# The last token block's norm of the convolution branch as a line of stages, and stores in part one given out some planned time behind their data

## The chip, the cores and the metric

The kernel runs on one core of one Trainium2 chip. The metric is the device time of one execution in microseconds, the median of several. The kernel before has a median of 2943.98 us in 3 runs (2941.24 to 2945.05). Engines are named as the profile names them: PE is TensorE, ACT ScalarE, DVE VectorE, POOL GpSimd, SP SyncE, which here only issues transfers (SPq in the timeline).

## The reference, cut to what matters

One layer of a streaming encoder works on 2048 prompt tokens and 64 sample tokens, 1024 channels wide:

```python
h = rms_norm(x, g1) * (1 + sc1) + sh1
z = h @ w_in                       # [GLU a | GLU b | q | k | v | gate conv | gate attn]
u = glu_a * sigmoid(glu_b)
conv = silu(layer_norm(depthwise31(u) + b_dw)) @ w_conv_out
attn = band_attend(rms_norm(q), rms_norm(k), v) @ w_attn_out
x = x + gt1 * ((sigmoid(g_conv) * conv + sigmoid(g_attn) * attn) @ w_o)
x = x + gt2 * swiglu(rms_norm(x, g2) * (1 + sc2) + sh2)
```

The change touches the layer norm with its swish on the convolution branch, the two sigmoid gates, and the attention result.

## The kernel before

**Part one** (0 to about 1163 us) makes `z` and both branches, **part two** multiplies by `w_conv_out`, `w_attn_out` and `w_o`, and the feed-forward network follows. Part one goes through four token blocks (0 to 576, 1088, 1600, 2112). In each of them PE makes, in this order, q, the convolution's first channel tile, k, the second, v, the third and fourth, and the gates (`g`). Activations and weights are split into a high and a low half in a rounded 32-bit type, so one product is a triple of matmuls: high by high, low by high, high by low. Everything that leaves for the chip's memory as an operand of a later product is therefore a pair of tiles, `part_h` and `part_l`. Pairs come from `parts()` (line 786), two buffers of each half for the whole of part one (NS = 2, line 781); plain temporaries come from `temp` (line 783), seven buffers.

PE's order in part one is the order of the code. The other work is written as generators that sit in lanes: normalising the next block, attention heads, the tail (layer norm) and the convolution. While the code issues PE's stages, a planner (`Stream`) adds up an estimated load for every engine, and each 500 ns of estimated PE time `tick` gives out what is due and then lets each lane take a step. `stream.when(engine)` is the planned time at which that engine has done its work so far; a generator that yields it isn't stepped before PE's planned time gets there. `stream.at(t, f)` runs `f`, here the issue of a store, when that time comes; `stream.flush()` runs all that is waiting, and the code calls it ahead of a new block's attention, in the last block ahead of the gates' last groups, and at the end of part one. So nothing but planned time decides where an instruction lands on its engine's in-order queue.

The rows of the profile all have line 105, since `Meter.run` records every call there; tiles tell them apart. Transfers keep their own lines:

- `conv_norm` (line 1296) takes a block's convolution output `y` through layer norm and swish, in four channel tiles of 128 x 512. Each is scaled by the deviation (POOL), goes through tanh into a tile `ln` (ACT), through two operations of DVE, and is split into a pair (ACT copies the high half, DVE or POOL subtracts for the low half). The pair is stored in `c_d` at line 1350. After each of these four steps the generator yields until the engine's planned time. It sits in the lane `tail`, for the last block added by the code at line 1706.
- `gates` (line 1354) takes the tanh of a gate column into a tile `gate` and stores it in `g_d` from ACT's own queue at once (line 1364).
- `finish_head` makes the attention result `o_p` of two heads, splits it and stores it in `o_d` (line 1460).
- In part two `merge` loads gate columns `tg` from `g_d` (line 1143) and operands `cin` from `c_d` and `o_d` (line 1151), makes 24 matmuls for each of eight channel tiles of the first 320 tokens (`ps<-cin`), and combines them on DVE (`t<-tg,ps`, then `ps<-ps,t`), four PSUM banks for all. The matmuls `pw` are the product with `w_o`. The pools of part two are opened when those of part one are closed (line 1716), and lie in the same memory: a first `t` must wait until the last store of part one has been read out.

In a head, PE makes scores (`sc`), DVE adds the bias (`pr<-sc,bias`), ACT takes the exponential, DVE the reciprocal, ACT scales, PE transposes (`ptp`), ACT and DVE split (`ph`, `pl`), and PE multiplies by the values (`po<-ph,vv`).

All other stores and all weight loads of part one go through SP's one in-order queue: a transfer whose data isn't there holds up everything issued behind it.

Of the kernel before, what the change touches and what calls it, by code (L numbers as in the profile page):

```python
# [8 lines left out]
F32 = mybir.dt.float32  # L9
# [23 lines left out]
QB = 512  # L33
# [18 lines left out]
FIRST_LAG = 14000.0  # L52
BIAS_LAG = 6000.0
OUT_LAG = 4000.0
CACHE_LAG = 16000.0
HEADS_NS = 2000.0
SIDE_G = 10
# [565 lines left out]
def streaming_layer(ctx: ExitStack, tc: tile.TileContext, I, O):  # L623
# [669 lines left out]
                )  # L1293
            yield

    def conv_norm(y, c0, n, t0):
        yv = y[:, :, c0 : c0 + n]
        yield lambda: not conv.gens
        s = wk.tile([P, 512], F32, tag="ln_s", bufs=1)

        def total():
            ps = ps_g.tile([P, 512], F32, tag="gp", name="pm")
            pe.matmul(ps[:, :n], ones, s[:, :n], start=True, stop=True)
            return ps

        gps.tensor_tensor(s[:, :n], yv[:, 0], yv[:, 1], ALU.add)
        for ct in (2, 3):
            gps.tensor_tensor(s[:, :n], s[:, :n], yv[:, ct], ALU.add)
        yield stream.when("pool") + PE_LAG
        pm = total()  # L1310
        yield stream.when("pe")
        for ct in range(4):
            dve.tensor_tensor(yv[:, ct], yv[:, ct], pm[:, :n], ALU.subtract)
        yield stream.when("dve")
        act.activation(s[:, :n], yv[:, 0], AF.Square)
        for ct in range(1, 4):
            tmp = temp("ln")
            act.activation(tmp[:, :n], yv[:, ct], AF.Square)
            yield stream.when("act")
            gps.tensor_tensor(s[:, :n], s[:, :n], tmp[:, :n], ALU.add)  # L1320
        yield stream.when("pool") + PE_LAG
        pm = total()
        yield stream.when("pe")
        act.activation(s[:, :n], pm[:, :n], AF.Sqrt, bias=eps_t)
        yield stream.when("act")
        for c in range(0, n, P):
            e = min(n, c + P)
            dve.reciprocal(s[:, c:e], s[:, c:e])
            yield
        yield stream.when("dve")  # L1330
        done = []
        for ct in range(4):
            gps.tensor_tensor(yv[:, ct], yv[:, ct], s[:, :n], ALU.mult)
            done.append(stream.when("pool"))
        for ct in range(4):
            yield done[ct]
            tmp = temp("ln")
            act.activation(tmp[:, :n], yv[:, ct], AF.Tanh, bias=lnh[:, 4 + ct : 5 + ct], scale=lnh[:, ct : ct + 1])
            yield stream.when("act")
            dve.tensor_scalar(yv[:, ct], yv[:, ct], lng[:, ct : ct + 1], lnb[:, ct : ct + 1], ALU.mult, ALU.add)  # L1340
            dve.scalar_tensor_tensor(tmp[:, :n], tmp[:, :n], 1.0, yv[:, ct], ALU.add, ALU.mult)
            yield stream.when("dve")
            hi, lo = parts()
            act.activation(hi[:, :n], tmp[:, :n], AF.Copy)
            yield stream.when("act")
            name = low(hi[:, :n], lo[:, :n], tmp[:, :n], n, TT_LESS)

            def store(ct=ct, hi=hi, lo=lo):
                for l, a in enumerate((hi, lo)):
                    nc.sync.dma_start(c_d[l, ct, :, t0 : t0 + n], a[:, :n].bitcast(F32))  # L1350

            stream.at(stream.when(name), store)

    def gates(b, free):

        o = PBLOCKS[b][0]
        w = PBLOCKS[b][1] - o

        def part(g, ws, c0, c1):
            ps = columns(*ws, kts(hh), kts(hl), c0, c1)  # L1360
            t = temp("gate")
            stream.after("act", "pe")
            act.activation(t[:, : c1 - c0], ps[:, : c1 - c0], AF.Tanh, scale=0.5)
            nc.scalar.dma_start(g_d[g // 8, g % 8, :, o + c0 : o + c1], t[:, : c1 - c0])

        def pair(g):
            ws = [W.get(("in", 2560 + g * P, h)) for h in range(2)]
            return [[[w[l][:, k, e * P : e * P + P] for w in ws for k in range(4)] for l in range(2)] for e in range(2)]

        n = 16 - SPLIT_G if b + 1 < len(PBLOCKS) else 16  # L1370
        for g in range(0, n, 2):
            for e, ws in enumerate(pair(g)):
                for c in halves(0, w):
                    part(g + e, ws, *c)
                if e:
                    W.done()
                    W.done()
                yield g + e
        rest = [ws for g in range(n, 16, 2) for ws in pair(g)]
        for c0, c1 in ((0, w // 2), (w // 2, w)):  # L1380
            for i, ws in enumerate(rest):
                part(n + i, ws, c0, c1)
                if c1 == w and i % 2:
                    W.done()
                    W.done()
            free["columns"] = c1
# [56 lines left out]
    def finish_head(h, po, n, q0, key):  # L1443
# [10 lines left out]
        if i:  # L1454
# [4 lines left out]
                for l, a in enumerate((hi, lo)):  # L1459
                    nc.sync.dma_start(o_d[l, h // 2, :, q0 : q0 + n], a[:, :n].bitcast(F32))  # L1460

            stream.at(stream.when("dve"), store)

    def spans(b):

# [182 lines left out]
    for b, stage in ORDER:  # L1648
# [44 lines left out]
        else:  # L1693
# [7 lines left out]
            if stage == 3:  # L1701
# [1 line left out]
                    tail.add(conv_norm(y, 0, SMP, 0))  # L1703
                    tail.add(conv_norm(y, SMP + HIST, QB, SMP))
                else:
                    tail.add(conv_norm(y, 0, QB, lo))
        for _ in range(MODS.get((b, stage), 0)):
            next(mods)
    next(mods)
# [672 lines left out]
```

## Time and profile before

| | us |
|---|---|
| median of 3 runs | 2943.98 (2941.24 to 2945.05) |
| the profiled execution | 2941.67 |
| its span, first to last instruction | 2939.5 |
| mean granted clock of PE in it | 0.997 |
| PE idle in the span | 50.2 |

The profiled execution lies 2.3 us under the median and 2.2 us above its own span. In a timeline a row has the start, the duration, the engine, line, operation, out<-in with the tiles' names, the shape, and in brackets how long the engine had been idle before it and what released it. A row of the stretch view has the stretch, its length, the busy time of PE, of PE's weight loads, of DVE, ACT and POOL (with counts), the granted clock of PE as a share of the full one, the share of the transfer engines and GB/s. In the view of waits a row has the waiting engine, tile and line, what it waited for, the total, the count and the longest. A row of the transfer view has the count, the size and the us from issue to landing.

### The profile page before, as it was taken

To read this page: it belongs to the slowest core of one execution; us is meant where nothing else is said; L and a number is where in the kernel's file an instruction comes from. 1 tells how busy PE (TensorE), PEld (TensorE's weight loads), DVE (VectorE), ACT (ScalarE), POOL (GpSimd) and SP (SyncE) were. 2 spreads that over 40 slices of the span, in tenths; PEclk is the share of its full clock that TensorE was granted. 3 is DMA by queue.
4 is the path that set the end of the run, shared out by engine and by line. 5 is a ranking of instruction groups with operands and counts; after the bars stand their busy time and mean duration, and the time that the engine had idled before them with its cause. 6 is when DMAs were issued, how large, how long until landed. Compare 5 with 4: busy or idle time off the path is not lost.

```text
span 2939.5 us, 44832 instructions
## 1 busy us (share of the span) xinstructions
PE 2889.3 (98%) x16193; PEld 2587.5 (88%) x16193; DVE 2053.9 (70%) x3648; ACT 1362.7 (46%) x2453; POOL 1164.9 (40%) x753
## 2 busy tenths in 40 slices
PE   7999999999999999999999999999999999999999
PEld 5899777888888887988999998999999999999998
DVE  5897788668967885577777756666666557566666
ACT  3346543751564266563444345444444345444442
POOL 1201210111011002553566452366567742465667
PEclk9999999999999999999999999999999999999999
DMA  9989899978996987984444875332333965333333
GB/s 322 315 305 314 287 281 329 285 232 306 285 297 197 320 270 224 291 295 157 144 144 146 292 261 200 97 122 94 115 115 104 346 220 179 97 103 106 115 107 127
DMA packets 467067, 628.04 MB, mean 214 GB/s; under 512 B 36196, under 2 KB 314584, under 8 KB 466845
## 3 DMA queue, kind: packets, MB, share of 16 engines
q1 hardware_dynamic: 452944, 606.11, 63.4%
q10 hardware_dynamic: 13901, 19.08, 1.9%
q8 instruction: 127, 2.08, 0.3%
q14 instruction: 95, 0.78, 0.1%
HBM read 476.53 MB, written 148.54 MB: 213 GB/s over the span
## 4 chain that ended last, share of the span: by engine, by line
PE 47%; DVE 2%; ACT 1%; DMA 1%; issue 1%; POOL 0%; SPq 0%; ACTq 0%; DVEq 0%; POOLq 0%
PE ps L105 29%; PE pd L105 13%; PE pw L105 5%; DVE wlo L105 1%; ACT whi L105 1%; DVE ps L105 0%; DMA cin<-o_d 0%; DMA x<-x_d 0%; DVE acc L105 0%; ACT xn L105 0%; DMA wst<-in_w_ffn_in 0%; DMA wfo<-in_w_ffn_out 0%; DMA tg<-g_d 0%; DVE sums L105 0%; PE pt L105 0%
## 5 line engine op out<-in xcount | busy, mean ns | idle before, releaser
L105 PE MATMUL ps<-t,whi 128*128 128x384 f32 (+1 forms) x2112 | 502.0, 322 | 2.8 <-ACT u L105 1.7
L105 POOL TENSOR_TENSOR wlo<-wst,whi 128x1024 fp32r<-128x1024 f32 (+1 forms) x159 | 362.7, 2293 | 246.1 <-ACT whi L105 214.4
L105 ACT ACTIVATE whi<-wst 128x1024 fp32r<-128x1024 f32 (+1 forms) x265 | 258.3, 979 | 316.1 <-PE ps L105 129.6
L105 PE MATMUL ps<-b,whi 128*128 128x384 f32 (+1 forms) x1584 | 380.7, 325 | 6.4 <-DVE v L105 2.1
L105 PEld LDWEIGHTS ps<-t,whi 128*128 128x128 f32 x2112 | 367.8, 188 | 10.1 <-ACT u L105 3.9
L105 DVE SCALAR_TENSOR_TENSOR y<-u,wd,y 128x512 f32<-128x512 f32 (+1 forms) x480 | 370.1, 774 | 8.0
L105 PE MATMUL ps<-hh,whi 128*128 128x512 f32 (+2 forms) x992 | 362.8, 366 | 0.1
L105 DVE TENSOR_TENSOR acc<-acc,pd 128x512 f32<-128x512 f32 x482 | 322.2, 685 | 48.1 <-PE pd L105 45.6
L105 PE MATMUL ps<-hh,wlo 128*128 128x512 f32 (+2 forms) x992 | 345.2, 348 | 0.0
L105 PE MATMUL ps<-hl,whi 128*128 128x512 f32 (+2 forms) x992 | 344.5, 347 | 0.0
L105 PE MATMUL ps<-t,wlo 128*128 128x384 f32 (+1 forms) x1056 | 338.5, 321 | 0.0
L105 PE MATMUL pd<-whi,hid 128*128 128x512 f32 x912 | 297.9, 391 | 0.6 <-DVE hid L105 0.3
L105 PEld LDWEIGHTS ps<-b,whi 128*128 128x128 f32 x1584 | 276.9, 188 | 14.6 <-DVE v L105 3.2
L105 ACT ACTIVATE pr<-pr,sm 128x640 f32<-128x640 f32 (+3 forms) x272 | 201.9, 749 | 137.1 <-DVE sm L105 134.8
L105 PE MATMUL ps<-b,wlo 128*128 128x384 f32 (+1 forms) x792 | 256.1, 323 | 0.0
L105 POOL TENSOR_TENSOR r<-t,mhalf 128x1 f32<-128x1 f32 (+2 forms) x68 | 82.3, 1219 | 403.7 <-DVE t L105 377.8
L105 PEld LDWEIGHTS ps<-hh,wlo 128*128 128x128 f32 x992 | 186.5, 188 | 22.6
L105 DVE TENSOR_TENSOR wlo<-wst,whi 128x1024 fp32r<-128x1024 f32 (+1 forms) x106 | 135.9, 1286 | 100.3 <-ACT whi L105 98.9
L105 PEld LDWEIGHTS pd<-whi,hid 128*128 128x128 f32 x912 | 171.2, 188 | 37.2 <-DVE acc L105 1.8
L105 PEld LDWEIGHTS ps<-hh,whi 128*128 128x128 f32 x992 | 187.0, 189 | 18.2 <-issue 3.3
L105 PEld LDWEIGHTS ps<-hl,whi 128*128 128x128 f32 x992 | 187.4, 189 | 14.3 <-issue 1.7
L105 PEld LDWEIGHTS ps<-t,wlo 128*128 128x128 f32 x1056 | 198.2, 188 | 0.8
(233 smaller groups left out, 6309.6 us busy)
## 6 DMA issues: line engine op xcount, KB each, us to landing
whi<-w_din_h SPq DMA_DIRECT2D x72, 512.0 KB, 6.4
wlo<-w_din_l SPq DMA_DIRECT2D x72, 512.0 KB, 7.3
wst<-sum_d SPq DMA_DIRECT2D x131, 256.0 KB, 3.1
wfo<-in_w_ffn_out SPq DMA_DIRECT2D x64, 512.0 KB, 4.1
wmod<-in_w_ada SPq DMA_DIRECT2D x46, 512.0 KB, 8.8
sum_d<-ws SPq DMA_DIRECT2D x88, 256.0 KB, 2.0
wst<-in_w_ffn_in SPq DMA_DIRECT2D x85, 256.0 KB, 3.2
wst<-in_w_in SPq DMA_DIRECT2D x40, 512.0 KB, 6.0
```

Source lines behind the costliest of these rows:

```text
L105: self.last = f(*args, **kw)
```

## The change

Three things are done, and no operation is added or taken away.

1. `conv_norm` of the **last block** runs as a line: seven steps with one yield each, in which channel tile i is scaled (POOL), tile i - 1 goes through tanh (ACT), tile i - 2 through DVE's two operations, and tile i - 3 is split and stored. The other blocks keep the old order.
2. The stores of `c_d`, and of `o_d`, are due 2000 ns of planned PE time later than before (`PART_LAG`).
3. The gates' stores on ACT's queue, formerly issued at once, are due 2000 ns after ACT's planned time.

```diff
@@ -52,6 +52,7 @@
 FIRST_LAG = 14000.0
 BIAS_LAG = 6000.0
 OUT_LAG = 4000.0
+PART_LAG = 2000.0
 CACHE_LAG = 16000.0
 HEADS_NS = 2000.0
 SIDE_G = 10
@@ -1293,7 +1294,7 @@
                 )
             yield
 
-    def conv_norm(y, c0, n, t0):
+    def conv_norm(y, c0, n, t0, line=False):
         yv = y[:, :, c0 : c0 + n]
         yield lambda: not conv.gens
         s = wk.tile([P, 512], F32, tag="ln_s", bufs=1)
@@ -1328,28 +1329,55 @@
             dve.reciprocal(s[:, c:e], s[:, c:e])
             yield
         yield stream.when("dve")
+        tmps = [None] * 4
+
+        def over(ct):
+            gps.tensor_tensor(yv[:, ct], yv[:, ct], s[:, :n], ALU.mult)
+
+        def swish(ct):
+            tmps[ct] = temp("ln")
+            act.activation(tmps[ct][:, :n], yv[:, ct], AF.Tanh, bias=lnh[:, 4 + ct : 5 + ct], scale=lnh[:, ct : ct + 1])
+
+        def times(ct):
+            tmp = tmps[ct]
+            dve.tensor_scalar(yv[:, ct], yv[:, ct], lng[:, ct : ct + 1], lnb[:, ct : ct + 1], ALU.mult, ALU.add)
+            dve.scalar_tensor_tensor(tmp[:, :n], tmp[:, :n], 1.0, yv[:, ct], ALU.add, ALU.mult)
+
+        def give(ct):
+            tmp = tmps[ct]
+            hi, lo = parts()
+            act.activation(hi[:, :n], tmp[:, :n], AF.Copy)
+            if not line:
+                yield stream.when("act")
+            name = low(hi[:, :n], lo[:, :n], tmp[:, :n], n, TT_LESS)
+
+            def store():
+                for l, a in enumerate((hi, lo)):
+                    nc.sync.dma_start(c_d[l, ct, :, t0 : t0 + n], a[:, :n].bitcast(F32))
+
+            stream.at(stream.when(name) + PART_LAG, store)
+
+        if line:
+            for i in range(7):
+                if 0 <= i - 3:
+                    yield from give(i - 3)
+                for step, ct in ((times, i - 2), (swish, i - 1), (over, i)):
+                    if 0 <= ct < 4:
+                        step(ct)
+                if i < 6:
+                    yield stream.when("act", "dve", "pool")
+            return
         done = []
         for ct in range(4):
-            gps.tensor_tensor(yv[:, ct], yv[:, ct], s[:, :n], ALU.mult)
+            over(ct)
             done.append(stream.when("pool"))
         for ct in range(4):
             yield done[ct]
-            tmp = temp("ln")
-            act.activation(tmp[:, :n], yv[:, ct], AF.Tanh, bias=lnh[:, 4 + ct : 5 + ct], scale=lnh[:, ct : ct + 1])
+            swish(ct)
             yield stream.when("act")
-            dve.tensor_scalar(yv[:, ct], yv[:, ct], lng[:, ct : ct + 1], lnb[:, ct : ct + 1], ALU.mult, ALU.add)
-            dve.scalar_tensor_tensor(tmp[:, :n], tmp[:, :n], 1.0, yv[:, ct], ALU.add, ALU.mult)
+            times(ct)
             yield stream.when("dve")
-            hi, lo = parts()
-            act.activation(hi[:, :n], tmp[:, :n], AF.Copy)
-            yield stream.when("act")
-            name = low(hi[:, :n], lo[:, :n], tmp[:, :n], n, TT_LESS)
-
-            def store(ct=ct, hi=hi, lo=lo):
-                for l, a in enumerate((hi, lo)):
-                    nc.sync.dma_start(c_d[l, ct, :, t0 : t0 + n], a[:, :n].bitcast(F32))
-
-            stream.at(stream.when(name), store)
+            yield from give(ct)
 
     def gates(b, free):
 
@@ -1361,7 +1389,10 @@
             t = temp("gate")
             stream.after("act", "pe")
             act.activation(t[:, : c1 - c0], ps[:, : c1 - c0], AF.Tanh, scale=0.5)
-            nc.scalar.dma_start(g_d[g // 8, g % 8, :, o + c0 : o + c1], t[:, : c1 - c0])
+            stream.at(
+                stream.when("act") + PART_LAG,
+                lambda: nc.scalar.dma_start(g_d[g // 8, g % 8, :, o + c0 : o + c1], t[:, : c1 - c0]),
+            )
 
         def pair(g):
             ws = [W.get(("in", 2560 + g * P, h)) for h in range(2)]
@@ -1459,7 +1490,7 @@
                 for l, a in enumerate((hi, lo)):
                     nc.sync.dma_start(o_d[l, h // 2, :, q0 : q0 + n], a[:, :n].bitcast(F32))
 
-            stream.at(stream.when("dve"), store)
+            stream.at(stream.when("dve") + PART_LAG, store)
 
     def spans(b):
 
@@ -1703,7 +1734,7 @@
                     tail.add(conv_norm(y, 0, SMP, 0))
                     tail.add(conv_norm(y, SMP + HIST, QB, SMP))
                 else:
-                    tail.add(conv_norm(y, 0, QB, lo))
+                    tail.add(conv_norm(y, 0, QB, lo, b == len(PBLOCKS) - 1))
         for _ in range(MODS.get((b, stage), 0)):
             next(mods)
     next(mods)
```

Where instructions land follows from the planner. A first place is **PE at the end of part one**, around the last scores. `sc` are scores of a head, `ps<-hh,whi` and the like triples of gate columns, `gates_c` a small transpose, `ptp` the transposes of a softmax. Before:

```order
L105 MATMUL sc<-kk,q_12193 128x320 x4
L105 MATMUL ps<-hh,whi 128x512
L105 MATMUL ps<-hl,whi 128x512
L105 MATMUL ps<-hh,wlo 128x512
L105 MATMUL ps<-hh,whi 128x512
L105 MATMUL ps<-hl,whi 128x512
L105 MATMUL ps<-hh,wlo 128x512
L105 MATMUL ps<-hh,whi 128x512
L105 MATMUL ps<-hl,whi 128x512
L105 MATMUL ps<-hh,wlo 128x512
L105 MATMUL ps<-hh,whi 128x512
L105 MATMUL ps<-hl,whi 128x512
```

The last of the twelve gate matmuls behind `sc`, then `gates_c` and twelve `ptp` follow these rows. Of the change:

```order
L106 MATMUL sc<-kk,q_12190 128x320 x4
L106 MATMUL ps<-hh,whi 128x512
L106 MATMUL ps<-hl,whi 128x512
L106 MATMUL ps<-hh,wlo 128x512
L106 MATMUL ps<-hh,whi 128x512
L106 MATMUL ps<-hl,whi 128x512
L106 MATMUL ps<-hh,wlo 128x512
L106 MATMUL sc<-kk,q_12190 128x320 x4
L106 MATMUL pt<-ident,gates_c 32x128
L106 MATMUL ptp<-ident,pr 128x128 x12
L106 MATMUL po<-ph,vv 128x512
```

Gate columns that stood behind the last `sc` stand ahead of it now; the two groups of scores have six gate matmuls between them, and `ptp` follows the second with only `gates_c` between.

The second place is **SP at the end of part one**: stores of the norm (`c_d`), of attention (`o_d`), loads of weights for part two (`wst`) and of gate columns (`tg`). Before:

```order
L1350 DMA c_d<-part_h 128x512
L1350 DMA c_d<-part_l 128x512
L1350 DMA c_d<-part_h 128x512
L384 DMA wst<-in_w_o 128x1024
L915 DMA gt_d<-row 32x128
L384 DMA wst<-in_w_o 128x1024
L1460 DMA o_d<-part_h 128x512
L1460 DMA o_d<-part_l 128x512
L1350 DMA c_d<-part_l 128x512
L1350 DMA c_d<-part_h 128x512
L1143 DMA tg<-g_d 128x320
L1350 DMA c_d<-part_l 128x512
```

Of the change:

```order
L1356 DMA c_d<-part_h 128x512
L1356 DMA c_d<-part_l 128x512
L1356 DMA c_d<-part_h 128x512
L1356 DMA c_d<-part_l 128x512
L1356 DMA c_d<-part_h 128x512
L1356 DMA c_d<-part_l 128x512
L385 DMA wst<-in_w_o 128x1024 x2
L916 DMA gt_d<-row 32x128
L1491 DMA o_d<-part_h 128x512
L1491 DMA o_d<-part_l 128x512
L1144 DMA tg<-g_d 128x320 x2
L385 DMA wup<-in_w_conv_out 128x4x128
```

The three c_d stores that stood behind the o_d pair or a weight load are all ahead now, and the o_d pair is part one's last; a `tg` load that stood between c_d stores stands behind it.

The third place is **SP at the seam from block 0 to block 1**: four pairs of the first blocks' norm (`c_d`), weights of the value projection (`whi`, `wlo` from w_dqkv_3) and of the next product (w_din), values (`vv`) and queries (`q_d`). Before:

```order
L1350 DMA c_d<-part_h 128x512
L1350 DMA c_d<-part_l 128x512
L1350 DMA c_d<-part_h 128x512
L1350 DMA c_d<-part_l 128x512
L479 DMA whi<-w_dqkv_3_h 128x1024
L1350 DMA c_d<-part_h 128x512
L1350 DMA c_d<-part_l 128x512
L479 DMA wlo<-w_dqkv_3_l 128x1024
L1350 DMA c_d<-part_h 128x512
L1350 DMA c_d<-part_l 128x512
L1436 DMA vv<-v_d 128x4x128
L1054 DMA q_d<-part_h 128x4x128
```

Of the change:

```order
L1356 DMA c_d<-part_h 128x512
L1356 DMA c_d<-part_l 128x512
L480 DMA whi<-w_dqkv_3_h 128x1024
L480 DMA wlo<-w_dqkv_3_l 128x1024
L1356 DMA c_d<-part_h 128x512
L1356 DMA c_d<-part_l 128x512
L1467 DMA vv<-v_d 128x4x128
L1356 DMA c_d<-part_h 128x512
L1356 DMA c_d<-part_l 128x512
L1356 DMA c_d<-part_h 128x512
L1356 DMA c_d<-part_l 128x512
L480 DMA whi<-w_din_h 128x1024
```

The second, third and fourth pair have moved behind both weight loads of the value projection, the third and fourth behind `vv` too.

## The prediction, made before the changed kernel ran

> **What bounds the kernel now.** I begin with the page's first part, to see whether any engine sets the end by itself.
>
> ```profile
> PE 2889.3 (98%) x16193; PEld 2587.5 (88%) x16193; DVE 2053.9 (70%) x3648; ACT 1362.7 (46%) x2453; POOL 1164.9 (40%) x753
> ```
>
> TensorE (PE) is busy for 2889.3 of a span of 2939.5 us, so all its waits together are 50.2 us, and the change alters no matmul. It can gain only from those waits and from a slow clock behind them. The view of PE's waits says whom it waited for.
>
> ```profile
> PE pt L105 <- DVE kn L105: 6.1, 2, 4.0
> PE ps L105 <- DVE t L105: 5.8, 5, 3.4
> ```
>
> The longest of each kind (4.0 and 3.4 us) lie at the two seams where the moved stores stand: the seam from token block 0 to block 1, and the seam from part one to part two. The timeline of PE, for both:
>
> ```profile
> 360.51 0.63 PE L105 MATMUL pt<-ident,kn 128*128 128x128 f32 x4 [3.96 <-DVE kn L105]
> ...
> 1152.59 0.74 PE L105 MATMUL sc<-kk,q 128*128 128x320 f32 x4
> 1153.17 0.39 PE L105 MATMUL ps<-hh,whi 128*128 128x512 f32 x1
> ...
> 1155.92 0.27 PE L105 MATMUL pt<-ident,gates_c 128*32 128x128 f32 x1
> ...
> 1157.02 1.20 PE L105 MATMUL ptp<-ident,pr 128*128 128x128 f32 x9 [0.50 <-ACT pr L105]
> ...
> 1164.57 0.56 PE L105 MATMUL ps<-cin,whi 128*128 128x320 f32 x2 [1.40 <-DVE o_p L105]
> ...
> 1171.57 0.31 PE L105 MATMUL ps<-cin,wlo 128*128 128x320 f32 x1
> ...
> 1175.29 0.90 PE L105 MATMUL ps<-cin,whi 128*128 128x320 f32 x2 [3.42 <-DVE t L105]
> ...
> 1201.09 0.40 PE L105 MATMUL pw<-whi,m 128*128 128x512 f32 x1
> ```
>
> The stretch view gives the granted clock behind such waits.
>
> ```profile
> 20.00:24.00 4.00, 3.87 (x28) 1.22 (x28) 2.04 (x4) 0.00 (x0) 0.00 (x0) 1.00 1.08 358
> ...
> 109.40:114.40 5.00, 5.00 (x26) 4.25 (x27) 5.00 (x7) 3.02 (x4) 0.00 (x0) 1.00 0.91 312
> ...
> 361.00:366.00 5.00, 5.00 (x19) 4.21 (x18) 2.71 (x6) 1.72 (x4) 0.00 (x0) 0.56 1.10 379
> 366.00:371.00 5.00, 5.00 (x24) 4.27 (x23) 4.54 (x10) 1.41 (x2) 0.00 (x0) 0.76 1.04 399
> ...
> 1175.30:1180.30 5.00, 5.00 (x19) 5.00 (x20) 2.88 (x7) 0.44 (x1) 0.00 (x0) 0.50 0.90 269
> ```
>
> The third number from the right is the clock. After the wait of 3.96 it was 0.56 and then 0.76, after that of 3.42 it was 0.50. So a long wait is paid twice: 5.0 x 0.44 + 5.0 x 0.24 = 3.4 us more at the first seam, 5.0 x 0.50 = 2.5 us more at the second. Two shorter or earlier waits cost nothing more:
>
> ```profile
> 20.13 1.08 PE L105 MATMUL pa<-wmod,cl 128*32 128x256 f32 x8 [3.44 <-DMA wmod<-in_w_ada]
> ...
> 109.40 0.63 PE L105 MATMUL pt<-ident,kn 128*128 128x128 f32 x4 [2.15 <-DVE kn L105]
> ```
>
> The clock stayed at 1.00 behind 2.15 and, at the start, behind 3.44. The point from which it falls thus lies above 2.15 and about 3.4, and is not sharp.
>
> **The second seam, before.** Part two's first tiles lie in the memory of part one's, so VectorE's `t` waits for part one's last store to land. SyncE's rows (SPq), VectorE's (DVE) and GpSimd's (POOL) in one timeline:
>
> ```profile
> 1154.52 0.32 SPq L1350 DMA_DIRECT2D c_d<-part_h  x1
> ...
> 1164.67 0.55 DVE L105 TENSOR_SCALAR y<-y,cols 128x512 f32<-128x512 f32 x1 [0.15 <-ACT ln L105]
> 1165.25 0.69 DVE L105 SCALAR_TENSOR_TENSOR ln<-ln,y 128x512 f32<-128x512 f32 x1
> ...
> 1166.57 0.32 SPq L1460 DMA_DIRECT2D o_d<-part_l  x1
> ...
> 1169.43 2.39 POOL L105 TENSOR_TENSOR wlo<-wst,whi 128x1024 fp32r<-128x1024 f32 x1 [5.71 <-ACT whi L105]
> 1169.59 2.79 DVE L105 TENSOR_TENSOR part_l<-ln,part_h 128x512 fp32r<-128x512 f32 x1 [0.70 <-DMA o_d<-part_l]
> 1172.40 0.32 SPq L1350 DMA_DIRECT2D c_d<-part_l  x1
> ...
> 1174.75 0.49 DVE L105 SCALAR_TENSOR_TENSOR t<-tg,ps 128x320 f32<-128x320 f32 x1 [2.38 <-DMA c_d<-part_l]
> ...
> 1185.56 0.50 DVE L105 SCALAR_TENSOR_TENSOR ps<-tg,ps 128x320 f32<-128x320 f32 x1 [4.17 <-DMA tg<-g_d]
> ...
> 1192.88 0.49 DVE L105 SCALAR_TENSOR_TENSOR t<-tg,ps 128x320 f32<-128x320 f32 x1 [1.52 <-DMA tg<-g_d]
> ```
>
> The last c_d store is issued at 1172.40, because its VectorE subtraction ran only at 1169.59 and for 2.79 us. By the DMA view it lands 2.0 us after its issue:
>
> ```profile
> c_d<-part_l SPq DMA_DIRECT2D x1, 256.0 KB, 2.0
> ```
>
> 1172.40 + 2.0 = 1174.4, then `t`, then PE at 1175.29.
>
> **What the change does there.** With the pipelined norm all c_d pairs of the last block stand on SyncE ahead of both o_d stores, as the order rows of the section on the change show, and the o_d pair becomes the last store. But the code order of PE moves too: the planner issues the gate columns earlier, so behind the last score product (`sc`) stands only `gates_c`, where twelve column matmuls stood (1153.17 to 1155.92). PE's total work up to `gates_c` is unchanged, so the last `sc` ends at about 1155.9 instead of 1153.3. The softmax that follows it:
>
> ```profile
> 1153.37 0.82 DVE L105 CUSTOM_DVE_ANT_0 pr<-sc,bias 128x640 f32<-128x640 f32 x1 [0.55 <-PE sc L105]
> ...
> 1154.40 0.81 ACT L105 ACTIVATE pr<-pr,sm 128x640 f32<-128x640 f32 x1
> ...
> 1155.33 0.16 DVE L105 RECIPROCAL sm<-sm 128x1 f32<-128x1 f32 x1 [1.13 <-ACT pr L105]
> 1156.16 0.81 ACT L105 ACTIVATE pr<-pr,sm 128x640 f32<-128x640 f32 x1
> ...
> 1160.23 1.05 ACT L105 ACTIVATE whi<-wst 128x1024 fp32r<-128x1024 f32 x1
> ```
>
> Bias, exponential, reciprocal and scale: 0.82 + 0.81 + 0.16 + 0.81 with hand-overs is 3.0 us. Two of these chains now run close behind each other on ScalarE (ACT), which also turns out a gate between them: I take 3.5. The transposes (`ptp`) start at 1155.9 + 3.5 = 1159.4 instead of 1157.02: **+2.4**, the new idle being 0.50 + 2.4, or about 3 us in two pieces around three early transposes. Between `ptp` and the first column product lie 1164.57 - 1157.02 = 7.55 us; in it ScalarE no longer has a 1.05 us weight copy and a tanh among its copies, for which I take off half the copy, 0.55. Columns start at 1159.4 + 7.0 = 1166.4: **+1.8**.
>
> The release: in the old order o_d's low half was issued 2.0 us behind the start of the columns (1166.57 - 1164.57), with two of the norm's operations (0.55 + 0.69) ahead of its subtraction. Those are gone, so it is issued at about 1167.7, lands 2.0 to 3.0 later, and frees the memory at about 1170.2 instead of 1174.75. PE has two channel tiles of columns before it needs that, 1164.57 to about 1171.7, or 7.1 us: until 1173.5. The wait of 3.42 goes, **-3.4**, and with it the slow spell, **-2.5**. What is late next are the gates' loads (`tg`): their waits ended 10.8 and 18.1 us after the release (1185.56 and 1192.88 less 1174.75), so now at 1181.0 and 1188.3. Columns of the third and fourth channel tile are done at 1166.4 + 14.2 = 1180.6, of the fifth and sixth at 1187.7: waits of about 0.5 each, **+1.0**. Six of eight early output products (`pw`) move behind the columns, at no cost. Sum at this seam: 1.8 - 3.4 - 2.5 + 1.0 = **-3.1**. Its bounds: if the softmax costs 3.0 flat and no `tg` wait shows, -4.6; if POOL's 2.39 falls on the last subtraction again (2.79 for 0.68, +2.1 on the release, hence on both `tg` waits), -1.0.
>
> [...]
>
> **The first seam.** PE waits there for `kn`, behind a key pair that waits for a c_d store of the norm to leave one of the two part buffers. The store stood behind SyncE's wait for a late part:
>
> ```profile
> 355.52 0.61 ACT L105 ACTIVATE part_h<-ln 128x512 fp32r<-128x512 f32 x1
> ...
> 356.16 0.32 SPq L1350 DMA_DIRECT2D c_d<-part_h  x1
> ...
> 358.26 0.69 ACT L105 ACTIVATE part_h<-pt,gqk 128x512 fp32r<-128x512 f32 x1 [1.10 <-DMA c_d<-part_h]
> ```
>
> The third pair's store left at 356.16 and landed at 358.2 (it ends that wait). In the new order two weight loads of 128 x 1024 floats (`whi`, `wlo`, 512 KB each) and the second pair pass ahead of it, and ScalarE makes the third part some 3 us earlier. It is then given out near 353 to 354, behind about 2 MB at the 379 to 399 GB/s of the stretches above, 5 us, less what has drained by then: landed at about 357.7, 0.5 earlier. I take **-0.5**. Bounds: the first pair, behind two weight loads, took
>
> ```profile
> c_d<-part_h SPq DMA_DIRECT2D x1, 256.0 KB, 7.1
> ...
> c_d<-part_h SPq DMA_DIRECT2D x1, 256.0 KB, 4.6
> ```
>
> 7.1, a later one 4.6. With 7.1 from 353.9 the store lands at 361.0, 2.8 later than before: +2.8. If the wait falls under the clock's point, -0.5 and the 3.4 of slow clock: -3.9.
>
> The other moved stores (o_d and the gates' g_d in part one, 2 us of planned PE time later) start none of the long waits of PE listed above, and PE, not a buffer, sets the pace between them: 0. If a ring of two were tight at one of them, that one would cost up to its 2 us.
>
> **Sum.** -3.1 - 0.5 = -3.6 on the profiled execution's 2941.67: 2938.1. That execution is 2.3 under the median of the runs, 2943.98, so for the median 2940.4.
>
> **Rivals.** (A) The first seam's wait, 3.96 less 0.5, comes to 3.46, right at the point: if the clock holds, 3.4 more goes: 2937.0. For it: 1.00 behind 3.44 at the start; against: 0.50 behind 3.42 at the second seam. [...]
>
> (B) The first seam loses: stores behind 1.5 MB of weights land like the first pair (7.1). +2.8 for -0.5: 2943.7. For it: DMA share 1.10 and 1.04 there; against: 4.6 for a pair behind one load.
>
> (C) **Slower.** The uncovered softmax lowers the clock at 1159.4. The chain of 7.0 us up to the columns is part PE's and part ScalarE's and VectorE's; at half clock it takes at most 7 us more, and I take 4. The clock stays low until 5 us into the dense columns: 2.5. Columns then start at 1170.4, no `tg` wait shows, and the seam gives +1.8 + 4.0 + 2.5 - 3.4 - 2.5 = +2.4 instead of -3.1: 2945.9 with the first seam's -0.5. It decides whether the two pieces around the three transposes count as one wait of over 3.4. For it: 0.50 behind 3.42; against: 1.00 behind 2.15. With B's loss as well: 2949.2.
>
> That the change doesn't do what it says is small: the order rows have the c_d stores ahead of the o_d stores.
>
> **How the numbers follow.** Forecast 0.50, A 0.18, B 0.15, C 0.17. The time is that of the likeliest, 2940.4. The low end is A with the second seam's bound (1.5 better) and 2 us for the spread of the runs shown (2941.24 to 2945.05), 2933.5; the high end is C with 1.6 of that spread, 2947.5. About 0.2%, 5.9 us, is what a measurement can tell from no change: faster means under 2938.1, slower above 2949.9. A and a fifth of the forecast's spread give faster 0.27; C with B, slower 0.06; same 0.67.
>
> **What would show it.** Right: no wait <-DVE t over 1 us near 1173 and clock 1.00 there; a wait <-ACT pr of 2 to 3 us near 1159; last c_d store on SyncE before the o_d pair; first column product near 1166.4, last near 1196. At block 1, kn's wait 3.2 to 3.6. Wrong, if the clock is below 1 between 1160 and 1170, if kn's wait is over 5, or if a later ring of two parts opens a wait that PE does not have now.

## The result, and the profile after

The changed kernel takes 2947.28 us (median of 22 runs, 2943.2 to 2955.68), the kernel before 2943.66 in the 22 runs beside them (2940.12 to 2946.64). The ratio is 1.0015, with a 95% interval of 1.001 to 1.0021: **slower** by some 4 us, where 3.6 faster was forecast. (The interval lies wholly above 1, but 0.15% is less than the 0.2% that the prediction took as the least that can be told from no change.) The profiled execution has a span of 2944.0 us against 2939.5.

PE works as before; the page and the view of waits say so first.

```profile
PE 2888.1 (98%) x16193; PEld 2585.5 (88%) x16193; DVE 2051.1 (70%) x3648; ACT 1362.6 (46%) x2453; POOL 1163.6 (40%) x753
```
```profile
PE pa L106 <- DMA wmod<-in_w_ada: 7.0, 6, 2.7
...
PE pt L106 <- DVE kn L106: 5.3, 2, 3.1
PE pt L106 <- DVE x_t L106: 5.0, 2, 3.7
...
PE ptp L106 <- ACT pr L106: 3.1, 3, 2.4
...
PE po L106 <- DVE pl L106: 1.6, 2, 1.4
...
PE ps L106 <- DVE t L106: 1.3, 3, 1.0
```

The waits for `kn` and `t` have shrunk as forecast (from 6.1 to 5.3 and from 5.8 to 1.3 in all), and `ptp` has its wait of 2.4 for the softmax. But two waits are new at this length, for `x_t` and `pl` (no single one above 0.3 in the first profile of the kernel before), and one has grown at its place, for `wmod` (0.56 before, near 467; the 2.7 of the view is at the kernel's start). PE's timeline shows where:

```profile
276.31 0.29 PE L106 MATMUL po<-pl,vv 64*128 64x64 f32 x1 [1.37 <-DVE pl L106]
...
323.46 0.63 PE L106 MATMUL pt<-ident,x_t 128*128 128x128 f32 x4 [3.69 <-DVE x_t L106]
...
366.33 1.09 PE L106 MATMUL pt<-ident,kn 128*128 128x128 f32 x4 [3.14 <-DVE kn L106]
...
472.88 0.64 PE L106 MATMUL pa<-wmod,cl 128*32 128x256 f32 x8 [1.98 <-DMA wmod<-in_w_ada]
...
1166.47 0.33 PE L106 MATMUL ptp<-ident,pr 128*128 128x128 f32 x1 [2.44 <-ACT pr L106]
...
1175.42 0.56 PE L106 MATMUL ps<-cin,whi 128*128 128x320 f32 x2 [1.40 <-DVE o_p L106]
...
1197.87 0.56 PE L106 MATMUL ps<-cin,whi 128*128 128x320 f32 x2 [0.96 <-DVE t L106]
```

The stretch view (clock third from the right) shows what the clock made of four of them:

```profile
278.00:282.00 4.00, 4.00 (x23) 4.00 (x23) 1.74 (x5) 2.38 (x7) 0.72 (x1) 0.67 1.06 402
...
366.00:371.00 5.00, 4.67 (x19) 4.00 (x20) 2.97 (x8) 1.72 (x4) 0.00 (x0) 0.66 1.02 308
...
476.00:481.00 5.00, 4.73 (x25) 2.99 (x18) 0.84 (x2) 0.00 (x0) 0.00 (x0) 0.50 1.03 407
...
1166.00:1170.00 4.00, 3.14 (x15) 2.28 (x16) 1.81 (x3) 2.73 (x5) 0.00 (x0) 0.77 0.57 179
1170.00:1175.40 5.40, 3.82 (x21) 3.12 (x19) 2.15 (x4) 1.78 (x4) 0.00 (x0) 0.86 0.00 0
```

A wait of 1.37 among small matmuls was followed by a clock of 0.67 (276 us), and the pieces 1.98, 0.61 and 0.69 by 0.50 (472 us). Narrower stretches show what the shares in between are made of:

```profile
1168.10:1171.50 3.40, 3.40 (x13) 2.42 (x12) 2.14 (x4) 1.65 (x4) 0.00 (x0) 0.50 0.18 72
1171.60:1175.00 3.40, 2.22 (x16) 1.82 (x14) 1.35 (x3) 1.19 (x2) 0.00 (x0) 1.00 0.00 0
```

Here 0.77 and 0.86 are one low spell of 3.4 us at 0.50, cut by the edges of two stretches. In the same way the clock is 0.51 from 277.2 to 280.6 and 1.00 behind it, 0.50 from 366.0 to 369.4 and 1.00 behind it, and 0.50 from 475.2 to 482.0. So a share such as 0.67 depends on where the stretch was cut.

How much each place costs is read by matching PE's instructions in two traces: the n-th matmul of each kind in the one against the n-th in the other, and the difference of their starts, the shift against the profile of before. Its change over a place is that place's cost with the clock's part in it. In us, for this kernel and for those of the next section:

| over (us of before) | after | lags_only | lag_cd | lag_od | lag_od2 | lag_gd | line_only2 | before_again |
|---|---|---|---|---|---|---|---|---|
| 260 to 285, `pl` | +2.8 | +3.0 | 0.0 | 0.0 | 0.0 | +1.5 | 0.0 | 0.0 |
| 312 to 321, `x_t` | +3.6 | +2.9 | +5.5 | 0.0 | 0.0 | 0.0 | 0.0 | 0.0 |
| 322 to 371, `kn` | -3.8 | -3.3 | -3.4 | -1.4 | -1.5 | +2.3 | -0.1 | -2.8 |
| 460 to 481, `wmod` | +2.4 | +2.4 | -1.9 | +2.5 | +2.4 | -1.5 | -0.6 | -1.5 |
| 1085 to 1210, second seam | -1.6 | -1.8 | -0.4 | -0.1 | -0.2 | +0.1 | -1.4 | -1.4 |

The last column is the unchanged kernel in a second profile. The first 40 us alone differ by -0.4 to +2.9 between executions whose instructions are the same there. Nor are other places quiet: between 285 and 312 the unchanged kernel shifted by +1.9, with a low spell of the clock from 307.0 to 310.4 (128x288 matmuls of 0.44 us in it, of 0.29 to 0.30 behind it). So a figure of 1 to 3 us in one column is not a cost by itself, and the columns can't simply be added up to the medians; what counts is a wait that comes back with an edit and is absent without it.

### The profile page after: what moved, and what is told of

It is laid out like the page before. It is cut to its first block, busy times and chain, and to the rows that moved or that the text cites. A ratio compares the mean times of both kernels' runs of the same rounds, so it can differ in the third digit from the quotient of the medians.

```text
span 2944.0 us, 44834 instructions
## 1 busy us (share of the span) xinstructions
PE 2888.1 (98%) x16193; PEld 2585.5 (88%) x16193; DVE 2051.1 (70%) x3648; ACT 1362.6 (46%) x2453; POOL 1163.6 (40%) x753
## 4 chain that ended last, share of the span: by engine, by line
PE 48%; DVE 2%; ACT 1%; issue 1%; DMA 0%; POOL 0%; ACTq 0%; DVEq 0%
PE ps L106 29%; PE pd L106 14%; PE pw L106 5%; DVE wlo L106 1%; ACT whi L106 0%; DVE ps L106 0%; DVE acc L106 0%; DVE sums L106 0%; DMA tg<-g_d 0%; DVE pw L106 0%; ACT xn L106 0%; PE pt L106 0%; DVE t L106 0%; ACT hid L106 0%; DVE hid L106 0%
```

## The experiments

Theory 1 was that the late stores cost and the line gains; theory 2 that the line costs, by its uncovered softmax, and the stores are free.

**Parts of the change alone.** `line_only` and `line_only2` (one kernel, measured twice):

```diff
-            stream.at(stream.when(name) + PART_LAG, store)
+            stream.at(stream.when(name), store)
...
-            stream.at(
-                stream.when("act") + PART_LAG,
-                lambda: nc.scalar.dma_start(g_d[...], t[...]),
-            )
+            nc.scalar.dma_start(g_d[...], t[...])
...
-            stream.at(stream.when("dve") + PART_LAG, store)
+            stream.at(stream.when("dve"), store)
```

> The last block's norm as a line; the three kinds of stores are given out as before. Theory 1 (the late stores cost, the line gains): nothing before 1100 us, no wait for DVE x_t near 323 and none for DVE pl near 276; at the second seam the time gained is 1.5 to 3, so the time is 1.5 to 3 us under the kernel before. Theory 2 (the line costs, its uncovered softmax and the clock behind it, the stores are free): 3 to 4 us above the kernel before, all of it between 1150 and 1200.

> The line alone once more, since its interval (0.9999 to 1.0017) holds both signs. If the second seam gains the 2.8 us that its first profile showed between 1100 and 1201: 1 to 3 us under the kernel before. If that was one execution's luck with the clock: within 1 us or above.

Measured: 1.0008 (0.9999 to 1.0017) and 0.9994 (0.9985 to 1.0003). The line alone is neither a gain nor a loss that can be told: the first interval excludes the gain of theory 1 (1.5 to 3 us, 0.9995 to 0.9990), the second the loss of theory 2 (3 to 4 us, 1.0010 to 1.0014).

`lags_only` keeps the old norm in the last block as well, and `lag_cd`, `lag_od` and `lag_gd` keep one of the three late stores each; `lag_od2` is `lag_od` again:

```diff
-                    tail.add(conv_norm(y, 0, QB, lo, b == len(PBLOCKS) - 1))
+                    tail.add(conv_norm(y, 0, QB, lo))
```

> All three kinds of stores late by 2000 ns, the last block's norm in its old order. Theory 1: the waits of the changed kernel in part one stand again (pl near 276, x_t near 323, 3 to 4 us), the shift at 1100 us is +4 to +7, and it stays to the end: 4 to 7 us above the kernel before. Theory 2: within 1 us of the kernel before.

> Only the norm's stores c_d are late, nothing else of the change. If the late c_d stores hold the ring of two part buffers (x_t near 323 waits behind a part that waits for one): the wait of 3 to 4 us for x_t stands here, 3 to 5 us above the kernel before. If it is the late o_d stores: no such wait, within 1 us.

> Only the attention results' stores o_d are late. If the c_d stores hold the ring: within 1 us of the kernel before, no wait for x_t near 323. If the o_d stores do: that wait stands here and the time is 3 to 5 us above.

> Only the gates' stores g_d are late; PE's and nearly all of SP's order are as before, ACT's and DVE's differ in a few places. If these stores cause the wait for pl near 276 (which neither late c_d nor late o_d stores showed): po waits 1.4 us there, the clock falls behind it, some 3 us in all, and the time is 1 to 3 us above the kernel before. If that wait needs two kinds of late stores together: no wait there and within 1 us.

> All o_d stores late once more. If the wait for wmod belongs to the order of the stores: PE's first wait for wmod near 470 is 1.5 to 2.5 again and the clock behind it near 0.5. If it belongs to the one execution: 0.3 to 0.8. The time 0 to 3 us above the kernel before either way.

Measured: the three together 1.0018 (1.001 to 1.0027), so they carry the whole loss, as far as these intervals tell; c_d 1.0007 (0.9998 to 1.0016), o_d 1.0008 (1.0 to 1.0017) and again 1.0008 (0.9999 to 1.0017), g_d 1.0002 (0.9993 to 1.0011). None is clear by itself; their sum, 1.7 thousandths, is near that of the three together, but each term is uncertain by about 0.9. The table gives each its place. `pl` is g_d's: the wait stands in all four profiles with these stores late and in no other. `x_t` is c_d's. `wmod`'s longer wait is o_d's, twice; but the clock has a part in the +2.4, for `cd_prompt` (below), with no o_d store late and a first wait of 0.50, shifts by +1.2 there, its 128x512 matmuls taking 0.63 us from 473.6 to 477.2 and 0.39 behind that. With g_d alone late `kn` also waits 6.16 at the first seam, behind a c_d store that VectorE waited 3.41 for; why it landed so late is not shown, and `after`, with g_d late as well, has 3.14.

The `pl` wait is a matter of order. With g_d late, a piece of the sample tokens' norm stands ahead of the head's split on VectorE. Timeline of VectorE, `lag_gd` first, then the kernel before:

```profile
276.39 0.75 DVE L106 TENSOR_SCALAR y<-y,cols 128x64 f32<-128x64 f32 x1
277.17 1.16 DVE L106 SCALAR_TENSOR_TENSOR ln<-ln,y 128x64 f32<-128x64 f32 x1
278.25 0.21 DVE L106 TENSOR_TENSOR pl<-ptp,ph 64x64 fp32r<-64x64 f32 x1
```
```profile
272.41 0.22 DVE L105 TENSOR_TENSOR pl<-ptp,ph 64x64 fp32r<-64x64 f32 x1 [0.28 <-ACT ph L105]
272.75 0.32 DVE L105 TENSOR_SCALAR y<-y,cols 128x64 f32<-128x64 f32 x1
273.10 1.01 DVE L105 SCALAR_TENSOR_TENSOR ln<-ln,y 128x64 f32<-128x64 f32 x1
```

The `x_t` wait is a matter of the two part buffers. Timeline of `lag_cd`, SyncE, ScalarE and VectorE, with the wait that follows on PE, then the same store and VectorE's two operations in the kernel before:

```profile
306.76 0.53 SPq L1356 DMA_DIRECT2D c_d<-part_h  x1
...
312.19 1.46 SPq L515 DMA_DIRECT2D w_dqkv_h<-whi  x1
313.69 0.48 SPq L515 DMA_DIRECT2D w_dqkv_l<-wlo  x1
314.27 1.06 SPq L1356 DMA_DIRECT2D c_d<-part_h  x1
...
319.90 0.26 ACT L106 ACTIVATE part_h<-o_s 128x64 fp32r<-128x64 f32 x1 [0.97 <-DMA c_d<-part_h]
...
320.53 0.23 DVE L106 TENSOR_TENSOR part_l<-o_s,part_h 128x64 fp32r<-128x64 f32 x1 [2.53 <-DMA c_d<-part_l]
320.67 0.75 DVE L106 TENSOR_SCALAR x_t<-x_t,r 128x1024 f32<-128x1024 f32 x1
...
321.57 0.74 PE L106 MATMUL pt<-ident,x_t 128*128 128x128 f32 x4 [3.99 <-DVE x_t L106]
```
```profile
306.80 0.41 SPq L1350 DMA_DIRECT2D c_d<-part_h  x1
...
314.58 0.21 DVE L105 TENSOR_TENSOR part_l<-o_s,part_h 128x64 fp32r<-128x64 f32 x1
314.71 0.74 DVE L105 TENSOR_SCALAR x_t<-x_t,r 128x1024 f32<-128x1024 f32 x1
```

The fourth c_d pair of the sample tokens, issued at 306.80 before, now stands at 314.27 (this execution was 2.1 us late there already), behind two weight loads and two weight stores. ScalarE's `part_h<-o_s` waits 0.97 for the store of the high half, VectorE's subtraction `part_l<-o_s` waits 2.53 for the store of the low half, and the next block's scaled rows `x_t` stand behind the subtraction on VectorE. No run gave it a third buffer; that the buffer is the link is read from these rows.

**Which stores.** `cd_prompt` (measured twice) and `cd_sample` split the c_d stores by tokens; `cd_one4` makes one pair late, `od_one` and `od_67` one and two pairs of o_d. `after_cdp` is the whole change but for the sample tokens' c_d stores; in the others all else is as in the kernel before.

```diff
-            stream.at(stream.when(name) + PART_LAG, store)
+            stream.at(stream.when(name) + (PART_LAG if n == QB else 0.0), store)    # cd_prompt, after_cdp; cd_sample: n == SMP
...
+            c_made[0] += 1
+            stream.at(stream.when(name) + (PART_LAG if c_made[0] == 4 else 0.0), store)    # cd_one4
...
+            o_made[0] += 1
+            stream.at(stream.when("dve") + (PART_LAG if o_made[0] == 7 else 0.0), store)    # od_one; od_67: in (6, 7)
```

> Only the norm's stores of the prompt tokens (512 wide) are late; those of the 64 sample tokens, o_d and g_d are as before, and the last block keeps its old order. If the sample tokens' c_d stores hold the part buffers near 320: no wait for x_t there, while the wait for kn at the first seam still shrinks from 3.96 to about 3.1, and the clock behind it is better: 0 to 2.5 us under the kernel before. If any late c_d store costs: the same 2 us above as with all c_d stores late.

> Late c_d stores of the prompt tokens alone once more. If the edit itself gains: 1.5 to 4 us under the kernel before again. If the first measurement was a draw from runs that spread over 10 us: within 1 us on either side. In the profile the wait for kn is again about 4 (3.98 at the first look, so the gain is not there).

> Only the sample tokens' four c_d pairs are late, the complement of the kernel with the prompt tokens' pairs late. If they carry the loss of late c_d stores: PE waits 3.5 to 4 us for x_t near 320, the shift over that place is +4 to +5, of which the place of kn may give some back, and the time is 2 to 3 us above the kernel before, 3 to 6 above the prompt tokens' alone. If the loss at x_t is given back at the first seam (as the one pair alone showed): within 1 us of the kernel before.

> One pair of c_d stores alone is late, the fourth (of the sample tokens), which moves behind two pairs of weight loads and two of weight stores. If this pair holds one of the two part buffers: VectorE's queue stops at the part of the sample tokens' attention result, and PE waits 3 to 4 us for x_t near 320: 2 to 4 us above the kernel before. If late c_d stores cost by their number: under 1 us.

> The whole change, but the sample tokens' c_d stores are given out at once. If these four pairs make the wait for x_t in the whole change too: no wait for x_t near 323; waits for pl near 276 and for wmod near 472 stay; 1 to 3 us under the changed kernel, 2 to 3 above the kernel before. If the late o_d stores make that wait as well: it stays.

> One pair of o_d stores alone is late, the seventh, which the kernel before issues near 448 us ahead of the loads of the next head's queries and keys; it moves behind them, and not one other instruction moves on any engine. If it is this pair that makes the loads of wmod late: PE's first wait for wmod near 470 is about 2 instead of 0.2 to 0.6, the clock behind it falls to 0.5, and the shift over that place is about +2 where it is -1 to -2 without it: 1 to 3 us above the kernel before. If the queue's order is worth nothing there: no change.

> Two pairs of o_d stores are late, the sixth and the seventh (near 404 and 448 us before). If the loads of wmod are late by the backlog of both: PE's first wait for wmod is about 2, the clock behind it 0.5, and the shift from 440 to 500 is +2 where it is -1 to -1.5 without; 2 to 3 us above the kernel before. If it takes another pair still: a wait under 1 there, and within 1 us.

Measured: `cd_prompt` 0.9989 (0.998 to 0.9998) and 0.9992 (0.9984 to 1.0001), 2.6 and 2.2 us by medians; `cd_sample` 1.0006 (0.9995 to 1.0017); `cd_one4` 0.9992 (0.9984 to 1.0001); `after_cdp` 1.0011 (1.0002 to 1.002); `od_one` 1.0006 (0.9997 to 1.0015); `od_67` 1.0003 (0.9994 to 1.0012). Against the expectations, `cd_sample`, `od_one` and `od_67` show no loss that is clear, and `after_cdp`, without the `x_t` wait, lies only 0.4 thousandths under the changed kernel's 1.0015, which their intervals don't separate. In its profile the time of that wait is lost elsewhere: `sc` waits 2.02 for a softmax at 1031, and 481 to 1100 shifts by +4.0. So the wait is shown, but not what it is worth in the median.

The sample tokens' pairs make the `x_t` wait: it is 3.03 in `cd_sample`, 2.39 with the one pair of `cd_one4`, and absent in `cd_prompt` and in `after_cdp`. Yet `cd_one4` was not slower: against 2.2 us lost there it got 3.6 back at the first seam, where `kn` waits 3.10. Most of that is the clock's, since the unchanged kernel got 2.8 back there in its second profile with a wait of 4.01 and a clock of 0.66 and 1.00 behind it, where 0.56 and 0.76 had been. That corrects a second point. `kn` waits 3.98 and 4.52 with the prompt tokens' stores late, and 3.09 with the sample tokens' late. So the forecast's reason for the shorter `kn` wait, the third prompt pair leaving earlier, is not what shortened it. Why `cd_prompt` is faster is not shown by any one wait.

`wmod` is a matter of how far ahead its loads are issued. `od_one` moved one pair of o_d stores on SyncE, from 448 to 457, and not one other instruction. The loads stand behind that pair; beyond what this execution was late already they were issued 2.6 us later, but landed in 7.6 us where they had taken 10.0, and PE waited 0.73. The rows of PE and SyncE for the kernel before, `lag_od2` and `od_67`:

```profile
457.12 3.14 SPq L249 DMA_DIRECT2D wmod<-in_w_ada  x4
...
467.23 0.64 PE L105 MATMUL pa<-wmod,cl 128*32 128x256 f32 x8 [0.56 <-DMA wmod<-in_w_ada]
```
```profile
462.26 2.72 SPq L250 DMA_DIRECT2D wmod<-in_w_ada  x4
...
469.80 0.64 PE L106 MATMUL pa<-wmod,cl 128*32 128x256 f32 x8 [2.70 <-DMA wmod<-in_w_ada]
```
```profile
460.84 2.80 SPq L250 DMA_DIRECT2D wmod<-in_w_ada  x4
...
468.53 0.64 PE L106 MATMUL pa<-wmod,cl 128*32 128x256 f32 x8 [0.79 <-DMA wmod<-in_w_ada]
```

PE was ready 9.6 us behind the first issue before (467.23 - 0.56 - 457.12), 6.9 us behind it in `od_67` and 4.8 in `lag_od2`; the first load landed in 10.0, 7.6 and 7.4 us. The other profiles fall in with these: 7.0 and 7.1 us and waits of 0.73 and 0.59 in `od_one` and `after_cdp`, 5.0 to 5.6 us and waits of 1.97 to 2.42 in `after`, `lags_only` and `lag_od`, 8.5 to 9.7 us and at most 0.50 where no o_d store is late. One pair thus takes some 2.6 us of the lead, which the quicker landing makes good; all the pairs together take 4 to 5. Why `after_cdp`, which has them all late, lost only 2.5 stays open.

**The second seam.** `before_again` is the kernel before, unchanged. `line_cdp` is the line with late c_d stores for prompt tokens; `line_cdp_room` lets the last block's attention run further ahead as well:

```diff
                         attn.burst, attn.spacing = 2, 0.0
+                        attn.room = {"dve": 4000, "act": 5000}
```

> The kernel before once more, unchanged, for a second profile of it. If the wait of 3.42 us for t at the second seam belongs to the kernel: it stands here again, with the clock near 0.50 behind it. If it was one execution's (a VectorE subtraction that met GpSimd's by 0.2 us): a wait under 1 us there as in the kernels with late stores and the old norm, and a low clock somewhere between 1160 and 1175. The time is within 1 us of the kernel before.

> The line in the last block, and late c_d stores for prompt tokens only. If both parts gain each at its seam: 2 to 5 us under the kernel before, with kn's wait near 3.1, no x_t wait, and at the second seam no t wait over 1 near 1173. If the line costs what its uncovered softmax takes: 0 to 2 above.

> The line and late c_d stores for prompt tokens, and in the last block the attention may run further ahead (room 4000 and 5000 for VectorE and ScalarE in place of 3000 and 4000), so that nine gate matmuls stand behind the last scores again. If the uncovered softmax is what the line pays: PE's wait for pr near 1160 falls from 2.4 to under 1, the clock between 1160 and 1175 stays above 0.9, columns start 2 us earlier, and the time is 2 to 3 us under the same kernel without the room, 4 to 6 under the kernel before. If the seam is held by something else: within 1 us of the one without.

Measured: 1.0001 (0.9992 to 1.0009), 0.9991 (0.9983 to 1.0) and 0.9998 (0.9989 to 1.0007). `line_cdp` may just be a gain, since its interval ends at 1.0; the 4 to 6 us expected of the room did not come. The second profile of the unchanged kernel has no wait of 3.42 at the second seam. Its timeline, VectorE, GpSimd and SyncE:

```profile
1169.44 0.68 DVE L105 TENSOR_TENSOR part_l<-ln,part_h 128x512 fp32r<-128x512 f32 x1
...
1170.08 2.40 POOL L105 TENSOR_TENSOR wlo<-wst,whi 128x1024 fp32r<-128x1024 f32 x1 [7.26 <-ACT whi L105]
1170.15 0.32 SPq L1350 DMA_DIRECT2D c_d<-part_l  x1
...
1172.71 0.49 DVE L105 SCALAR_TENSOR_TENSOR t<-tg,ps 128x320 f32<-128x320 f32 x1 [2.59 <-DMA c_d<-part_l]
```
```profile
1173.26 0.56 PE L105 MATMUL ps<-cin,whi 128*128 128x320 f32 x2 [0.74 <-DVE t L105]
```

Here VectorE's subtraction was 0.64 us ahead of GpSimd's and took 0.68; in the first profile GpSimd was 0.16 ahead and it took 2.79. In `od_one`, with GpSimd ahead by 1.14:

```profile
1171.05 2.39 POOL L106 TENSOR_TENSOR wlo<-wst,whi 128x1024 fp32r<-128x1024 f32 x1 [5.71 <-ACT whi L106]
1172.19 1.80 DVE L106 TENSOR_TENSOR part_l<-ln,part_h 128x512 fp32r<-128x512 f32 x1 [1.68 <-DMA o_d<-part_l]
```

Of the thirteen profiles with the old order in the last block, three have a `t` wait of 3.42 to 3.45 (the first profile and `od_one`, with GpSimd first, and `lag_od2`), and ten one of 0.69 to 0.80 (`before_again`, with VectorE first, among them). In nine of those ten part of the first two channel tiles ran at a lower clock (128x320 matmuls of 0.46 to 0.47 us where the others take 0.31; a share of 0.87 and 0.79 from 1160 to 1170 in `before_again`), and they took 8.5 to 9.8 us instead of 7.0, so the time went another way (7.0 and 8.5 to 9.8 are counted to the start of the last of their matmuls). All ten also have a second wait for `t` two channel tiles on, of 0.86 to 2.91, which the three do not have, as in `od_67`:

```profile
1188.41 0.75 PE L106 MATMUL ps<-cin,whi 128*128 128x320 f32 x2 [2.91 <-DVE t L106]
```

Over the seam (1085 to 1210) the thirteen shift by -3.0 to +3.1 against the first profile, -0.5 in the mean; the five with the line and the old room by -2.8 to +1.3, -1.3 in the mean; the difference is smaller than the spread of either group.

The room gave its order: `ptp` waits 1.82 instead of 2.44 and 0.39, and the clock stays at 1.00 from 1155 to 1175. Its seam is -1.8, no better than `line_cdp` (-2.1): the time came back as a wait of 1.51 for a weight's high half (`whi`) among the columns.

```profile
1159.39 1.20 PE L106 MATMUL ptp<-ident,pr 128*128 128x128 f32 x9 [1.82 <-ACT pr L106]
...
1185.22 0.73 PE L106 MATMUL pw<-whi,m 128*128 128x512 f32 x2 [1.51 <-ACT whi L106]
```

## Why the prediction was wrong, step by step

- **"The other moved stores ... 0."** This is the step that failed. It argued from PE's long waits of the old order, in which none starts at such a store, and it listed o_d and g_d but not the c_d stores of the sample tokens. The late stores made three waits in part one: `pl` +2.8, `x_t` +3.6 and `wmod` +2.4 over their places in the changed kernel's profile, 8.8 us, of which the two seams gave 5.4 back (-3.8 and -1.6). In the runs the late stores alone cost 1.8 thousandths, some 5 us (`lags_only`). What each wait adds to a median is not shown. The bound of 2 us for one tight ring was too small, since a store moved past planned time is moved past whole transfers: the c_d pair went behind two weight loads and two weight stores, some 5 us of queue (314.27 - 306.80 less 2.1). A ring of two parts that opens a new wait was among the prediction's own signs of being wrong, and `x_t` is that wait. And g_d's cost, for which no queue or ring was in question, came from another order on VectorE.
- **The wait for `t` goes: right.** 3.42 is gone, and PE's next such wait is 0.96; in the forecast +1.0 for the gates' loads. Two sums behind that term don't come out as written: 1166.4 + 2.0 - 0.55 - 0.69 is 1167.2, not 1167.7 (measured, the store of the low half is issued 1.36 us behind the start of the columns, 1176.78 less 1175.42, so the 1.3 that was used was near), and the second of the two waits counts the first one's delay again, so 0.6 and not 1.0 follows from its times.
- **The uncovered softmax, +2.4: right.** 2.44 and 0.39 where 0.50 had been.
- **7.0 us from `ptp` to the columns: right at full clock only.** `line_only` needed 7.0 (1163.55 to 1170.57) with the clock at 1.00, the changed kernel 8.2 (1167.19 to 1175.42) with the clock at 0.77 and 0.86. That is rival C's mechanism, at 1.2 us and not at 4.0, and without the slow spell in the columns (1.00 from 1175.4 to 1180.4).
- **-3.4 and -2.5 at the second seam: the size was off.** The two terms belong to an execution in which VectorE's subtraction ran beside GpSimd's and took 2.79 where it takes 0.68. A wait for `t` of that execution's length stood in three of thirteen, so what the line can take away on average is less. Seam for seam the line is worth 0.8 (-1.3 against -0.5), not 3.1. That difference is inside the spread of either group, and the runs of the line alone (1.0008 and 0.9994) don't tell it from nothing. The bound of -1.0 "if POOL falls on the subtraction again" was applied to the kernel after; the one before needed it.
- **The first seam, -0.5 by an earlier third pair: right in sign, wrong in reason.** The wait did shrink to 3.14, just under the forecast's 3.2 to 3.6, and the clock was 0.66 for one stretch in place of 0.56 and 0.76; but it shrinks by the sample tokens' stores (3.09 in `cd_sample`). And the point "above 2.15 and about 3.4", on which rival A rested, is no such point: the clock fell to 0.50 behind 3.14 here (366.0 to 369.4), and to 0.51 behind 1.37 at 276 us (277.2 to 280.6). Nor is the 1.00 behind 3.44 at the start, which spoke for A, shown: the matmuls behind that wait took 1.08 us, as at a clock of 0.50 (last section).
- **The range** (to 2947.5) just holds the median, for reasons it didn't name: rivals B and C added were the only slow case, and neither is what happened.

## What to carry to other kernels

A store that was given out later on SyncE's queue was late here by what it was moved behind, and its buffer with it: one c_d pair some 5 us, and the operations that needed its two halves' buffers waited 0.97 and 2.53 for them. Price each moved store by the new neighbours in the order rows and by who takes the buffer next, also where the engine that sets the end has no wait today. Before a long wait in one profile becomes a term of a sum, take a second profile of the unchanged kernel: here it took the wait away (0.74 for 3.42), and with it most of the gain that was forecast.

## What was not expected of the hardware

The clock fell behind much shorter waits than 3.4 us, among small matmuls or where several waits follow each other: 0.67 behind one of 1.37, 0.50 behind pieces of 1.98, 0.61 and 0.69. In the kernel before it was already 0.50 from 470.9 to 474.2, behind pieces of 0.56, 0.62 and 0.69 alone; in `before_again`, behind 0.39, 0.62 and 0.71, it stayed at 1.00 from 465 to 475. And it held behind longer ones: at 1.00 from 319 to 329 around the 3.69 for `x_t` in the changed kernel, while in `cd_sample`, behind 3.03 for the same tile, 128x512 matmuls took 0.63 us from 319.2 to 323.1 and 0.39 to 0.40 from 323.8 on. At the start the stretch view has 1.00 from 20 to 24 behind 3.44 in the first profile, but that trace has no record of the clock before 23.7, and eight matmuls `pa<-wmod,cl` took 1.08 us in it at 20.13 and at 21.76, as in the changed kernel at 20.59 under a recorded 0.50 (17.8 to 24.6), and 0.64 at 24.51. In `before_again` they took 1.08 as well, behind 3.69, with 0.54 from 20 to 24. So a clock that held behind 3.44 is not shown. Behind `kn` at the first seam it was 0.56 and 0.76 in the one (3.96), 0.66 and 1.00 in the other (4.01). The same wait was answered differently from one execution to another: behind 1.37 for `pl` the clock was 0.67 in the changed kernel, and behind 1.36 in `lag_gd` 1.00 from 280 to 284. So PE at 98% busy still has several places where some 1.5 to 3 us are decided anew in each execution: the unchanged kernel's second profile differs from its first by +1.9, -2.8, -1.5 and -1.4 over four of them.
